# A projection kernel whose first two pairs of row tiles are loaded as four transfers of one tile each

## The chip, the core and the metric

The kernel runs on one core of a Trainium2 chip. The core has five engines that work side by side: TensorE (PE; its weight loads are shown apart as PEld), VectorE (DVE), ScalarE (ACT), GpSimd (POOL) and SyncE (SP), which here only issues transfers. Transfers are moved by 16 DMA engines that all queues of the core share. The metric is the device time of one execution in microseconds (us).

## The reference

The input x holds 16 x 512 = 8192 rows of 768 numbers, the weight `w_qkv` 768 rows of 2304 numbers, both in float32. The reference multiplies them and cuts the 2304 result columns into three parts of 768, which are stacked:

```python
qkv = np.matmul(x, w_qkv)
q, k, v = qkv[..., :768], qkv[..., 768:1536], qkv[..., 1536:]
return np.stack([q, k, v], axis=0).astype(np.float32)
```

So 25 MB of x and 7 MB of weight are read, and 75.5 MB of result are written.

## The kernel before

**Tiling.** The 8192 rows of x make 64 row tiles of 128 rows; two of them are a pair, p = 0 to 31. The contraction of 768 is cut into six slices j of 128 (`KT`), three of them being a half (`KH`). Of the 2304 result columns, two groups q = 0 and 1 have 2 x 512 columns each, and a remainder of 256 columns (`REM`) lies between them. TensorE multiplies 128 x 128 of x by 128 x 512 of weight into one bank of its accumulator memory (PSUM); there are eight banks.

**Most pairs** (2 to 31) are computed with a scheme of seven products for a 2 x 2 block matrix instead of eight, in part with float32 operands (`do`, `product`, line 247). For it x is loaded so that VectorE can turn it in blocks of 32 x 32 (`transpose`, line 155), and rounded to bfloat16 (`round_x`, `round_row`, line 203).

**Pairs 0 and 1** come first, while the weight is still arriving, and go another way. `load_rows` (line 159) loads a pair's x as it lies in memory, rows on partitions: tile `xin[p]` has 128 partitions, two row tiles r and 768 numbers of each. `cast_row` (lines 166 to 173) rounds one row tile to bfloat16, the first n columns on VectorE (line 167), the rest on ScalarE (line 168). `turn_row` turns it with six TensorE transposes (line 181), and `copy_row` (lines 188 and 190) copies a half of the turned tile from PSUM to `xb[p]`. `block` (line 485) then multiplies slice by slice: for weight slice j, the four row tiles of the two pairs, six slices for the first 512 columns and six for the next.

**Order.** The scheduling is by hand: each engine works through its instructions in the order of the program. Around the change this order is, in the program: 10 dummy matmuls on zeros (`busy(10)`, line 458); cast of pair 0's two row tiles; their transposes; a copy on VectorE; 2 dummy matmuls; cast of pair 1's two row tiles; their transposes; the cast of the first weight slice, shared by VectorE and ScalarE; copies; the cast of the second slice; more copies; casts of slices 2 to 5 on VectorE (line 465); then the first `block`.

SP issues the loads in this order: x of pair 0, x of pair 1, six weight slices of 256 KB for the first 512 columns (line 92), two weight blocks of 768 KB for the next 512, one part of pair 2's x, the remainder weight (768 KB), seven more parts of pair 2's x (line 137, 96 KB each), and more weight blocks. All of these go through one queue. The framework gives each transfer one of eight semaphores in turn, and a transfer is issued only when the one eight before it has landed. Each instruction that reads loaded data waits for the transfer that wrote that part of the tile.

Behind the first two blocks TensorE computes the remainder columns of pairs 0 and 1 (`rem`, line 310), for which VectorE and GpSimd round the remainder weight (lines 559 and 560), and then the first product of pair 2 (line 247).

Of the kernel before, what the change touches and what calls it, by code (L numbers as in the profile page):

```python
# [10 lines left out]
def kernel(  # L11
# [20 lines left out]
    nc = tc.nc  # L32
    P = 128
# [20 lines left out]
    x_flat = x.rearrange("b t h -> (b t) h")  # L54
# [66 lines left out]
    xin, xf, xb, sr = {}, {}, {}, {}  # L121
# [36 lines left out]

    def load_rows(p):
        xin[p] = xin_pool.tile([P, 2, K], fp32, name="xin")  # L160
        rows = x_flat[p * 2 * P:(p + 1) * 2 * P, :]
        nc.sync.dma_start(xin[p][:], rows.rearrange("(r m) k -> m r k", m=P))  # L162

    xc, turned_rows = {}, {}

# [274 lines left out]
    zero = xb_pool.tile([P, CB], bf16, name="zero", tag="xb")  # L440
    nc.vector.memset(zero[:], 0.0)
    load_rows(0)
    nc.scalar.activation(tiny[:], zero[:, :1], ident)
    make_identity(nc, eye)
    load_rows(1)
    load_blocks(0, 0, 1)
    load_blocks(0, 1)
# [257 lines left out]
```

## Time and profile before

Three runs took 358.91, 359.10 and 359.31 us, the median being 359.1. The profile is of the execution that took 359.31.

| what | value |
|---|---|
| time of the profiled execution | 359.31 us |
| its span (first to last instruction) | 357.5 us |
| TensorE busy | 352.4 us, 99% of the span |
| TensorE weight loads | 252.1 us, 71% |
| VectorE / ScalarE / GpSimd busy | 264.0 / 186.4 / 177.4 us |
| transfers | 108.10 MB, mean 302 GB/s |
| the two loads of pairs 0 and 1 | 768 KB each, median 4.9 us from issue to landing |
| issue of these two on SP | 0.44 and 0.45 us, from 0.74 and 1.25 us |

In the profile L162 is line 162 of the kernel. A line of the timeline gives start and length in us, engine, source line, operation, what it writes and reads, the shape and a count; in square brackets stands the idle time of the engine before it, and what ended that. In the chain that ended last, each step is the work that released the next one. A line of the table by windows gives a stretch of time and its length, the busy time and count of PE, PEld, DVE, ACT and POOL, the granted TensorE clock, the share of the DMA engines that was busy and the GB/s moved.

### The profile page before, as it was taken

The page shows a single profiled execution, that of the slowest core. Times are in us where ns is not written, and L with a number is a line of the kernel's source. Part 1 is how long each engine was busy: PE and PEld are TensorE (multiplying, and loading weights), DVE is VectorE, ACT ScalarE, POOL GpSimd, SP SyncE. Part 2 cuts the span into 40 slices and gives each one's busy share as a digit, 9 for nine tenths or more (in the row PEclk, how much of TensorE's full clock was granted, in tenths as well). Part 3 has the DMA queues.
Part 4 walks back from the last instruction along what each step waited for, and adds up shares of the span by engine and source line. Part 5 has one row for each costly group of instructions (what it writes and reads, how often), then busy time and mean ns, then how long its engine had stood idle before and what let it go on. Part 6 is the DMA issues. An engine that isn't in the chain of part 4 may idle for free.

```text
span 357.5 us, 5336 instructions
## 1 busy us (share of the span) xinstructions
PE 352.4 (99%) x1776; PEld 252.1 (71%) x1776; DVE 264.0 (74%) x309; ACT 186.4 (52%) x320; POOL 177.4 (50%) x184
## 2 busy tenths in 40 slices
PE   8999999999999999999999999999999999999996
PEld 3465577868777686877768777686877768777674
DVE  3689876796876959777695876959777695876743
ACT  5577754545454553645545454553645545454553
POOL 0031683376566353665535566353665535566320
PEclk9999999999999999999999999999999999999999
DMA  7997999998999798998979899798999979869497
GB/s 299 361 355 228 337 385 345 391 313 336 300 321 328 233 380 207 347 270 288 353 183 392 231 340 308 215 398 214 341 269 309 322 199 391 227 225 358 154 379 261
DMA packets 82075, 108.10 MB, mean 302 GB/s; under 512 B 4992, under 2 KB 62080, under 8 KB 82048
## 3 DMA queue, kind: packets, MB, share of 16 engines
q1 hardware_dynamic: 75088, 102.52, 85.7%
q10 hardware_dynamic: 6960, 5.24, 5.4%
q8 instruction: 14, 0.23, 0.3%
q14 instruction: 13, 0.11, 0.1%
HBM read 32.24 MB, written 75.50 MB: 301 GB/s over the span
## 4 chain that ended last, share of the span: by engine, by line
PE 93%; DMA 4%; SPq 1%; DVE 1%; ACT 0%; issue 0%; DVEq 0%
PE ps L247 79%; PE ps L310 11%; PE ps L485 3%; DMA xin<-in_x_dram 2%; DMA st<-in_w_qkv_dram 2%; SPq L137 1%; DVE xf L155 0%; SPq L92 0%; SPq L162 0%; ACT xb L203 0%; DVE orem L413 0%; ACT orem L412 0%; DVEq L155 0%
## 5 line engine op out<-in xcount | busy, mean ns | idle before, releaser
L247 PE MATMUL ps<-t,s 128*128 128x512 f32 x720 | 177.8, 395 | 0.0
L247 PEld LDWEIGHTS ps<-t,s 128*128 128x128 f32 x720 | 135.0, 188 | 29.6 <-ACT o L256 0.2
L155 DVE STREAM_TRANSPOSE xf<-xin 128x768 f32<-128x768 f32 (+1 forms) x45 | 93.4, 2078 | 2.7 <-DMA xin<-in_x_dram 2.6
L247 PE MATMUL ps<-b,xb 128*128 128x512 bf16 x360 | 85.4, 380 | 0.1
L287 DVE TENSOR_TENSOR o<-o,ps 128x512 f32<-128x512 f32 x56 | 38.5, 688 | 52.3 <-ACT o L286 51.7
L194 POOL CAST xb<-xf 128x1536 bf16<-128x1536 f32 x28 | 41.1, 1467 | 57.0 <-DVE xf L155 57.0
L214 POOL TENSOR_TENSOR s<-xf 128x384 fp32r<-128x384 f32 x29 | 31.0, 1067 | 72.5 <-DVE xf L155 70.8
L247 PEld LDWEIGHTS <-xb 128*128 128x128 bf16 x360 | 33.9, 98 | 37.0 <-issue 4.2
L293 DVE TENSOR_TENSOR o<-o,ps 128x512 f32<-128x512 f32 x60 | 41.2, 687 | 20.5 <-PE ps L247 19.4
L286 ACT ACTIVATE o<-ps 128x512 f32<-128x512 f32 x56 | 33.7, 601 | 41.9 <-PE ps L247 41.9
L247 PE MATMUL ps<-b,s 128*128 128x512 f32 x180 | 50.5, 389 | 0.0
L290 ACT ACTIVATE o<-ps 128x512 f32<-128x512 f32 x60 | 36.1, 601 | 25.0 <-PE ps L247 22.7
L367 DVE TENSOR_TENSOR o<-o,ps 128x512 f32<-128x512 f32 x78 | 47.8, 682 | 0.0
L310 PE MATMUL ps<-w_rem,xb 128*128 128x256 bf16 x384 | 47.5, 273 | 0.2 <-POOL w_rem L560 0.2
L275 ACT ACTIVATE o<-ps 128x512 f32<-128x512 f32 x60 | 36.1, 602 | 19.2 <-PE ps L247 13.9
L310 PEld LDWEIGHTS <-xb 128*128 128x128 bf16 x384 | 37.4, 98 | 11.9 <-issue 1.1
L324 ACT ACTIVATE orem<-ps 128x512 f32<-128x512 f32 x31 | 18.6, 598 | 48.2 <-PE ps L310 31.3
L247 PEld LDWEIGHTS ps<-b,s 128*128 128x128 f32 x180 | 33.8, 188 | 7.0
L215 POOL TENSOR_TENSOR s<-s,xf 128x384 fp32r<-128x384 f32 x29 | 29.6, 1021 | 2.3
L216 POOL TENSOR_TENSOR s<-xf 128x384 fp32r<-128x384 f32 x29 | 29.4, 1015 | 0.0
L218 POOL TENSOR_TENSOR s<-xf,s 128x384 fp32r<-128x384 f32 x29 | 29.2, 1008 | 0.0
L371 ACT ACTIVATE o<-ps 128x512 f32<-128x512 f32 x26 | 15.6, 600 | 18.1 <-PE ps L247 17.5
(51 smaller groups left out, 162.7 us busy)
## 6 DMA issues: line engine op xcount, KB each, us to landing
out_dram<-o SPq DMA_DIRECT2D x60, 768.0 KB, 4.6
out_dram<-o SPq DMA_DIRECT2D x75, 256.0 KB, 3.7
xin<-in_x_dram SPq DMA_DIRECT2D x88, 192.0 KB, 5.7
out_dram<-orem SPq DMA_DIRECT2D x31, 256.0 KB, 2.2
xin<-in_x_dram ACTq DMA_DIRECT2D x24, 192.0 KB, 4.4
st<-in_w_qkv_dram SPq DMA_DIRECT2D x5, 768.0 KB, 8.1
xin<-in_x_dram SPq DMA_DIRECT2D x2, 768.0 KB, 4.9
st<-in_w_qkv_dram SPq DMA_DIRECT2D x6, 256.0 KB, 5.9
```

The costliest lines, as they stand in the source:

```text
L155: nc.vector.transpose(turned[:, g:g + n], rows[:, g:g + n])
L194: nc.gpsimd.tensor_copy(out=xb[p][:], in_=xf[p][:])
L214: 1: lambda g: g.tensor_tensor(s[:, 1], a21, a22, op=add),
L215: 2: lambda g: g.tensor_tensor(s[:, 2], s[:, 1], a11, op=sub),
L247: nc.tensor.matmul(ps[:], lhs[j], rhs[j], start=(start and j == 0), stop=(j == KH - 1), skip_group_check=True,)
L275: nc.scalar.activation(c12, u.x[:], ident)
L286: nc.scalar.activation(c22, u.x[:], ident)
L287: nc.vector.tensor_tensor(c22, c22, u.y[:], op=add)
L290: nc.scalar.activation(c21, u.x[:], ident)
L293: nc.vector.tensor_tensor(c12, c12, u.y[:], op=add)
L310: nc.tensor.matmul(ps, xb[p][:, j, r * P:(r + 1) * P], w_rem[j // KH][:, j % KH, :], start=(j == 0), stop=(j == KT - 1), skip_group_check= ...
L367: dve.tensor_tensor(c, c, u.z[:], op=add)
```

## The change

`load_rows` issues one transfer for each of the two row tiles of a pair instead of one transfer for both. It is called for pairs 0 and 1, so that the queue begins with four transfers of 384 KB where it had two of 768 KB. The tile, its layout in memory, the bytes and the pieces of 3 KB that a row makes stay as they are; nothing else in the program is edited.

```diff
     def load_rows(p):
         xin[p] = xin_pool.tile([P, 2, K], fp32, name="xin")
-        rows = x_flat[p * 2 * P:(p + 1) * 2 * P, :]
-        nc.sync.dma_start(xin[p][:], rows.rearrange("(r m) k -> m r k", m=P))
+        for r in range(2):
+            row = (2 * p + r) * P
+            nc.sync.dma_start(xin[p][:, r], x_flat[row:row + P, :])
```

## The prediction, made before the result was known

> **What bounds the kernel now.** I read the page first, for the share of each engine:
>
> ```profile
> PE 352.4 (99%) x1776; PEld 252.1 (71%) x1776; DVE 264.0 (74%) x309; ACT 186.4 (52%) x320; POOL 177.4 (50%) x184
> ```
>
> TensorE is busy 99% of the span, so a gain must come from the few us in which it is not, or is busy with dummy work. The chain that ended last, asked for the first 24 us, says what sets the pace there:
>
> ```profile
> 2.25 5.90 DMA st<-in_w_qkv_dram
> ...
> 11.38 7.74 DMA xin<-in_x_dram
> ...
> 21.78 1.47 PE ps L247 x6
> ```
>
> The head is a transfer chain (columns: start, length, what): a weight load lands at 8.14, the queue goes on, a part of pair 2's x lands at 19.12, VectorE turns it from 19.24, ScalarE rounds it from 20.88, and at 21.78 TensorE starts pair 2. From there to the end the chain is TensorE alone, so the span of 357.5 is "when pair 2 starts" plus 335.7 us. TensorE's own timeline ahead of that point:
>
> ```profile
> 1.19 4.45 PE L458 MATMUL ps<-zero 128*128 128x512 bf16 x10 [1.19 <-DVE zero L441]
> 5.55 1.11 PE L181 MATMUL ps<-eye,xc 128*128 128x128 bf16 x12
> 6.50 0.59 PE L458 MATMUL ps<-zero 128*128 128x512 bf16 x2
> 7.39 0.85 PE L181 MATMUL ps<-eye,xc 128*128 128x128 bf16 x12 [0.30 <-ACT xc L168]
> 8.08 5.34 PE L485 MATMUL ps<-b,xb 128*128 128x512 bf16 x24
> ...
> 18.56 0.49 PE L310 MATMUL ps<-w_rem,xb 128*128 128x256 bf16 x3
> 19.25 2.45 PE L310 MATMUL ps<-w_rem,xb 128*128 128x256 bf16 x21 [0.19 <-POOL w_rem L560]
> ```
>
> The dummy matmuls end near 5.5, real ones start at 8.08 and run without a hole to 18.56; then come a wait of 0.19 for the converted remainder columns and one under 0.1 for pair 2. So the matmuls of the head also nearly touch: starting them earlier alone is worth nothing, since the remainder weight and pair 2's x hold the end of the stretch. Both must move. The other engine that matters is VectorE:
>
> ```profile
> 4.97 0.63 DVE L167 CAST xc<-xin 128x384 bf16<-128x384 f32 x2 [3.84 <-DMA xin<-in_x_dram]
> 6.36 0.36 DVE L190 COPY xb<-ps 128x384 bf16<-128x384 bf16 x1 [0.77 <-PE ps L181]
> 6.84 0.73 DVE L167 CAST xc<-xin 128x480 bf16<-128x480 f32 x2
> 7.50 0.31 DVE L167 CAST b<-st 128x288 bf16<-128x288 f32 x1
> 7.73 0.35 DVE L190 COPY xb<-ps 128x384 bf16<-128x384 bf16 x1
> ```
>
> Pair 0's x lands at 4.95 and pair 1's at 6.81. The copy at 7.73, whose end at 8.08 releases the first real matmul, stands behind the cast of the first weight slice (7.50), which starts as that slice lands. SP issues its next transfer at 7.50 too, after waiting 0.3 for the same landing. Last, transfer rates in quarter-microseconds:
>
> ```profile
> 2.00:2.25 0.25, 0.25 (x2) 0.15 (x1) 0.00 (x0) 0.22 (x2) 0.00 (x0) 1.00 0.63 221
> 2.25:2.50 0.25, 0.25 (x2) 0.06 (x1) 0.00 (x0) 0.00 (x0) 0.00 (x0) 1.00 0.55 209
> 2.50:2.75 0.25, 0.25 (x2) 0.09 (x1) 0.00 (x0) 0.00 (x0) 0.00 (x0) 1.00 0.87 258
> ...
> 33.50:33.75 0.25, 0.25 (x3) 0.11 (x2) 0.25 (x1) 0.25 (x2) 0.25 (x1) 1.00 0.88 292
> ```
>
> The last two columns are the share of the 16 DMA engines and GB/s. The first transfer needs some 0.75 us to bring the engines to 0.9; from 3 us on they are full, near 400 GB/s, until pair 2 is in.
>
> **The change, part by part.** *Transfers.* Two issues of 0.44 and 0.45 us (768 KB each) become four of 384 KB. SP's 256 KB weight loads cost about the same to issue (0.46), so I count 0.45 each with 0.05 between: SP is 1.0 us later at the first weight slice, 2.75 instead of 1.75. Cover: that slice's bytes lie behind 1.5 MB of x and flow only from about 6.8 (landing 7.48 less 0.65, the spacing of the slices), so 3.6 us remain between the end of its issue (3.2) and its turn. Without the cover it would cost the 1.0.
>
> *The queue's window.* The issues show eight transfers in flight: the ninth goes out at 4.96, just behind pair 0's landing, the tenth at 6.83 behind pair 1's, then one behind each weight slice. With four x transfers the ninth and tenth are the fifth and sixth slices, waiting for pair 0's two tiles (about 4.0 and 4.9); the two 768 KB blocks wait for pair 1's tiles (about 5.85 and 6.8). The second block so goes out as before, and pair 2's first part waits for the first slice, the remainder weight for the second, as now. All these bytes have a backlog of several us ahead of them, so nothing runs dry. Cost 0.
>
> *Landing of the tiles.* 384 KB takes about 0.95 us (pair 1 lands 1.87 behind pair 0). Row tile 0 of pair 0 lands at about 4.0 instead of 4.95, of pair 1 at 5.9 instead of 6.8; the second tiles as now. VectorE and ScalarE cast tile 0 a microsecond earlier. But the ten dummies hold TensorE until 5.43, against 5.55 for the first transpose now: 0.1 gained. Transposes of pair 1's first tile move from 7.39 to about 6.9, those of its second to about 7.3. Behind them VectorE still meets the weight slice at 7.50, and its copy still ends at 8.08. Two more casts now carry a wait of their own; what stands behind them on VectorE (the copy at 6.36) needs TensorE anyway. Gain on the path: 0. What is late next is that first weight slice.
>
> *The start of the stream.* This is the only part that can move the end, since every later landing to 19.2 follows it. Bounds: if the ramp is the time to hand out the first transfer's 256 pieces, halving it gives half the 0.9 us from the first packet to full rate, 0.45 earlier; if the ramp is a start-up of its own, 0; two more completions cost at most 0.1 (six 256 KB slices land 0.65 apart where 262,144 B at 400 GB/s need 0.655, so one completion is lost in rounding). The nearest row is the 96 KB load that meets an almost idle queue at 33.2: 128 pieces, as one tile would have, and it reaches 0.88 in about 0.5 us against 0.75. I take 0.2 earlier, between both ends.
>
> The Trainium skill ("DMA: Bandwidth & Descriptors", Rules for kernel authors and the fit in Anatomy of one DMA) says to batch transfers to 1 MiB, with about 2.0 us fixed per transfer on the software-generated path; were that paid in series here, two more transfers would give +4 us, about 363. The 0.65 spacing disagrees: the fixed part overlaps in the queue.
>
> **Sum.** The profiled execution took 359.31: 357.5 of span and 1.8 around it. Issue 0, window 0, casts 0, start of the stream -0.2; pair 2 then starts at 21.6, TensorE's 335.7 us follow. That is 359.1 against 359.31. The profiled run is the highest of the three shown, 0.2 above their median of 359.1, so I forecast 358.9.
>
> **Rivals.**
> 1. *The transfers are hidden and the stream starts as before.* For it: the later 768 KB store fills all engines quickly, so the slow ramp may belong to the first use of the queue. Time 359.1.
> 2. *The ramp goes with the number of pieces.* Then -0.45: 358.65. For it: the ramp of the 96 KB load is shorter; against: bytes per piece differ fourfold.
> 3. *Slower: TensorE's rate.* Ten dummies take 4.45 us, 24 equal matmuls at 8.08 take 5.34, so the array goes from 0.43 to 0.22 us each in this head. With earlier tiles the idle time moves: transposes, two dummies, a hole of 0.2, transposes, then 0.4 ahead of 8.08, where now there is one hole of 0.30. If that keeps the slow rate alive past 8.08, each slow matmul costs 0.21, less 0.27 for the two stalls that it eats; from five on it passes 0.2% (+0.8, about 359.9), eight give +1.4 (360.5). Against: the fast rate is there at 6.50 already, ahead of the moved holes. The Trainium skill ("TensorE: Matmul & The Clock Gate", The HAM clock gate) puts the change after a busy window of about 3.4 us and the fall back after an idle one; holes of 0.4 would not matter by it, and the row at 6.50 agrees.
> 4. *Slower: the issues reach the stream.* If SP's two further issues do delay the bytes, everything to 21.78 moves by 1.0: 360.1. It needs the 3.6 us of cover to be wrong.
> 5. *The change does not do what it says*, if the casts wait for the whole tile. The weight casts each wait for their own slice, so I expect not; 359.1 anyway.
>
> One edge lies later: ScalarE waits 2.2 us for a remainder store to land (32.9), and its backlog then reaches TensorE with almost no margin at 36 to 44 us. If TensorE comes 0.2 earlier and that landing does not, the gain is given back there (359.1); if the landing slips, up to 1 us is lost.
>
> **How the numbers follow.** Forecast (358.6 to 359.1 of its own) 0.42; rivals 1 and 5 0.27; rival 2 0.10; rival 3 0.08; rival 4 0.04; the later edge slipping 0.05; unknown 0.04, half of it faster. A measurement of this kernel tells about 0.2%, 0.7 us, from no change. Slower by more: rivals 3 and 4, part of the edge and unknown, 0.17. Faster by more needs a start 0.7 earlier than any row allows, or a lucky tail of rival 2: 0.07. Within: 0.76. The range goes from rival 2 with 0.25 for the spread of the runs, 358.4, to rival 3's point of decision, 359.9.
>
> **What would show it.** The first cast at about 4.0 or earlier; the first transpose at 5.45; SP at the first weight slice at 2.75, at pair 2's first part within 0.3 of 7.50; the first real matmul between 7.7 and 8.1; pair 2 at 21.4 to 21.8; nothing but TensorE behind. Wrong if slices land later than now, if matmuls behind 8.08 take over 0.3 us, or if new idle time appears on TensorE from 36 us on.

## The result, and the profile after

The changed kernel takes 360.65 us (median of six executions, 360.44 to 361.44) against 359.22 (six, 358.91 to 359.48): a ratio of 1.0044, 95% interval 1.0033 to 1.0055. The change costs some 1.4 us where no difference was forecast, and the time lies outside the predicted range. The profiled execution is the slowest of the six: 361.44, of which 359.7 are span, so its trace shows more than the usual loss, 2.1 us against the profiled execution of before.

The share of each engine, from the page, has hardly moved; TensorE's busy time is the same within 0.6 us (this trace holds 1757 of its 1776 matmuls):

```profile
PE 351.8 (98%) x1757; PEld 253.0 (70%) x1776; DVE 264.3 (73%) x309; ACT 186.3 (52%) x320; POOL 177.6 (49%) x184
```

The chain that ended last shows where (columns: start, length, what). It no longer goes through pair 2's x but through the weight loads:

```profile
2.60 0.43 SPq L92
...
3.08 6.92 DMA st<-in_w_qkv_dram
...
10.02 10.17 DMA str<-in_w_qkv_dram
...
20.24 1.22 POOL w_rem L561
...
21.51 2.45 PE ps L311 x21
...
24.01 1.24 PE ps L248 x5
```

SP issues the first weight slice at 2.60, a transfer chain follows until the remainder weight lands at 20.19, GpSimd rounds it, and pair 2 starts at 24.01 instead of 21.78. What follows has the very length it had before, 359.7 less 24.0 or 335.7 us, and in neither trace does TensorE wait there. (From 88 us on the chain now also names VectorE and GpSimd in places, where before it named TensorE alone; the length shows no cost of it.) So all of the loss arises ahead of 24 us. TensorE's timeline there (start, length, in square brackets the idle time before and what ended it):

```profile
1.19 4.45 PE L459 MATMUL ps<-zero 128*128 128x512 bf16 x10 [1.19 <-DVE zero L442]
5.43 1.49 PE L182 MATMUL ps<-eye,xc 128*128 128x128 bf16 x12
6.71 0.77 PE L459 MATMUL ps<-zero 128*128 128x512 bf16 x2
8.33 0.51 PE L182 MATMUL ps<-eye,xc 128*128 128x128 bf16 x6 [0.84 <-ACT xc L169]
9.28 0.51 PE L182 MATMUL ps<-eye,xc 128*128 128x128 bf16 x6 [0.44 <-ACT xc L169]
9.82 5.34 PE L486 MATMUL ps<-b,xb 128*128 128x512 bf16 x23
...
20.83 0.49 PE L311 MATMUL ps<-w_rem,xb 128*128 128x256 bf16 x3 [0.48 <-DVE w_rem L560]
```

The first transposes start at 5.43, earlier than before, but those of pair 1 wait 0.84 and 0.44 us for casts, and the first real matmul comes at 9.82 instead of 8.08. VectorE's timeline says what the casts waited for:

```profile
3.80 0.36 DVE L168 CAST xc<-xin 128x384 bf16<-128x384 f32 x1 [2.67 <-DMA xin<-in_x_dram]
4.71 0.36 DVE L168 CAST xc<-xin 128x384 bf16<-128x384 f32 x1 [0.56 <-DMA xin<-in_x_dram]
...
7.77 0.41 DVE L168 CAST xc<-xin 128x480 bf16<-128x480 f32 x1 [1.10 <-DMA xin<-in_x_dram]
8.72 0.41 DVE L168 CAST xc<-xin 128x480 bf16<-128x480 f32 x1 [0.54 <-DMA xin<-in_x_dram]
9.38 0.31 DVE L168 CAST b<-st 128x288 bf16<-128x288 f32 x1 [0.25 <-DMA st<-in_w_qkv_dram]
```

The two tiles of pair 0 arrive at 3.78 and 4.69, a little earlier than the whole of pair 0 did (4.95). The third tile, pair 1's first, comes only at 7.75, the fourth at 8.70, where the whole of pair 1 had come at 6.81; the first weight slice lands at 9.36 instead of 7.48. The reason stands in the table by windows (last columns: granted TensorE clock, share of the 16 DMA engines, GB/s), of after:

```profile
3.50:4.00 0.50, 0.50 (x3) 0.15 (x1) 0.20 (x1) 0.20 (x1) 0.00 (x0) 1.00 1.02 406
4.00:4.50 0.50, 0.50 (x2) 0.15 (x1) 0.16 (x1) 0.32 (x1) 0.00 (x0) 1.00 0.68 264
...
5.00:5.50 0.50, 0.50 (x3) 0.22 (x2) 0.07 (x1) 0.24 (x1) 0.00 (x0) 1.00 1.15 197
5.50:6.00 0.50, 0.50 (x7) 0.50 (x6) 0.00 (x0) 0.00 (x0) 0.00 (x0) 1.00 0.47 154
```

and the same stretch of before:

```profile
5.00:5.50 0.50, 0.50 (x2) 0.00 (x0) 0.50 (x2) 0.50 (x2) 0.00 (x0) 1.00 0.98 381
5.50:6.00 0.50, 0.50 (x6) 0.46 (x6) 0.10 (x1) 0.41 (x1) 0.00 (x0) 1.00 0.94 381
```

The stream is at full rate by 4.0 us and then breaks down until about 6.5. From 4.0 to 6.5 us it moved 0.61 MB where the kernel before moved 0.99, so 0.38 MB, or 0.95 us at 400 GB/s, are missing. The table counts a piece (the 3 KB of one row of x, for example) wholly in the window in which it starts, so its 1.15 and 0.47 have to be read together. Counted by the time that the pieces really fill, the 16 engines were occupied for 0.82 of these 2.5 us, before for all of it. So about half of what is missing is idle time of the engines, and the other half is pieces that took too long. Between 4.0 and 6.8 us the trace has 239 data pieces instead of 399. Their median is 121 ns in both, but nine took more than 400 ns, the longest 1304; before, none did. The landings of the 16 engines' shares of the third tile show the second part of the loss:

```
third tile, landing of each engine's share, us
5.42 5.43 5.46 5.47 5.48 5.49 5.50 5.57 5.58 5.70 5.73 6.29 6.38 6.47 6.67 7.75
```

Eleven engines are even earlier than the 5.9 predicted. One is 2 us late, and a transfer counts as landed when its last engine is through. This lag behind the next to last engine, 1.1 us here, stays at 0.7 to 0.9 us in every landing up to the second weight block's at 16.89. Loss of rate and lag together come to most of the 1.9 us by which the first weight slice is late.

### The profile page after: what moved, and what is told of

The parts are those of the page before. It is cut to its first block, busy times and chain, and to the rows that moved or that the text cites. A ratio compares the mean times of both kernels' runs of the same rounds, so it can differ in the third digit from the quotient of the medians.

```text
span 359.7 us, 5319 instructions
## 1 busy us (share of the span) xinstructions
PE 351.8 (98%) x1757; PEld 253.0 (70%) x1776; DVE 264.3 (73%) x309; ACT 186.3 (52%) x320; POOL 177.6 (49%) x184
## 3 DMA queue, kind: packets, MB, share of 16 engines
q10 hardware_dynamic: 6960, 5.24, 5.4%
## 4 chain that ended last, share of the span: by engine, by line
PE 70%; POOL 15%; DVE 6%; DMA 5%; issue 3%; SPq 1%; ACT 0%
PE ps L248 56%; PE ps L311 12%; DVE xf L155 5%; POOL xb L195 5%; POOL s L216 3%; POOL s L215 3%; POOL s L217 3%; PE ps L486 3%; DMA str<-in_w_qkv_dram 3%; DMA st<-in_w_qkv_dram 2%; SPq L163 0%; POOL w_rem L561 0%; DVE o L294 0%; SPq L92 0%; DVE orem L414 0%
## 5 line engine op out<-in xcount | busy, mean ns | idle before, releaser
L248 PE MATMUL ps<-b,xb 128*128 128x512 bf16 x343 | 81.5, 379 | 1.1
```

The costliest lines, as they stand in the source:

```text
L248: nc.tensor.matmul(ps[:], lhs[j], rhs[j], start=(start and j == 0), stop=(j == KH - 1), skip_group_check=True,)
```

## The experiments

Each is compared with the kernel before on the same chip. Names in capitals are the theories that the expectations weigh: PLACE, that the third transfer finds the engines short of work, whatever it is; SUPPLY, the same for two short transfers ahead of it; BACKLOG, that the transfers queued behind x get in its way; PATTERN, that the order in which a short transfer reads memory is to blame; COUNT, that there are more transfers; CASTS, that casts now run while x still arrives; ISSUE, that SP issues during these microseconds; CUSHION, that a stream which opens with short transfers stalls, and that a long one at its head prevents it.

### Which pair matters

The split for one pair alone.

```diff
-        rows = x_flat[p * 2 * P:(p + 1) * 2 * P, :]
-        nc.sync.dma_start(xin[p][:], rows.rearrange("(r m) k -> m r k", m=P))
+        if p == 0:
+            for r in range(2):
+                row = (2 * p + r) * P
+                nc.sync.dma_start(xin[p][:, r], x_flat[row:row + P, :])
+        else:
+            rows = x_flat[p * 2 * P:(p + 1) * 2 * P, :]
+            nc.sync.dma_start(xin[p][:], rows.rearrange("(r m) k -> m r k", m=P))
```

> Only pair 0 is loaded as two transfers of one row tile; pair 1 stays one transfer of 768 KB. In the changed kernel the first two tiles landed at 3.78 and 4.69 us and the third only at 7.75 instead of about 5.7. Theory PLACE (the third transfer, wanted at about 4.1 us, finds the engines short of work whatever it is): pair 1 lands 1 to 2 us late, at 7.5 to 8.5 instead of 6.6, and the time is 360 to 361. Theory PATTERN (a transfer of 128 rows that follow each other in memory is what stalls, in pair 1): as before, 358.8 to 359.3, pair 1 lands at 6.5 to 6.8. Theory COUNT (each additional transfer at the head of the queue costs its share): about 359.9, pair 1 at 7.2 to 7.5.

Measured: 361.56 us against 358.84, ratio 1.0060 (1.0028 to 1.0092). The five executions fall into two groups, 361.56 to 362.24 and 359.43 to 359.64. In the profiled one, of the upper group, pair 0's tiles land at 4.03 and 4.92; of pair 1's single transfer 15 engines are through by 6.90 and one at 8.69, after a piece that took 1125 ns at 5.10. So splitting pair 0 is enough for the whole loss, as PLACE had it, and the two groups suggest that it strikes in some executions and much less in others. In this trace nearly all of it is the lag of one engine: from 4.0 to 6.5 us the stream moved 0.95 MB, almost what it moved before.

The other pair, with `p == 1` in place of `p == 0`:

> Only pair 1 is loaded as two transfers of one row tile; pair 0 stays one of 768 KB. PLACE: the third transfer, pair 1's second tile, is wanted at about 5.2 us, and a second stands ready for the engines from 4.2; little or no stall, 359.0 to 359.6, tiles of pair 1 at 5.9 and 6.9. PATTERN: the stall of about 2 us is all here, 360.4 to 361.4, second tile at 8 to 8.7. COUNT: 359.9, second tile at 7.2 to 7.5.

Measured: 359.2 us, ratio 1.0006 (0.9997 to 1.0016): no difference. The tiles land at 4.95, 5.86 and 6.81, the first slice at 7.51. TensorE's timeline of this kernel:

```profile
7.09 0.85 PE L186 MATMUL ps<-eye,xc 128*128 128x128 bf16 x12
7.97 5.34 PE L490 MATMUL ps<-b,xb 128*128 128x512 bf16 x24
...
21.21 1.47 PE L252 MATMUL ps<-b,xb 128*128 128x512 bf16 x6
```

Transposes and matmuls follow each other without a wait, pair 2 starts at 21.21, and pair 1 lands as predicted for it (5.9, 6.8). The pair whose landing suffered in the changed kernel is not the pair whose split does the harm. With three transfers of x in both kernels, COUNT can't tell the one from the other.

### The pattern in memory

Four transfers of the same size, each of 64 partitions and both row tiles, so that the data come in the order of the kernel before.

```diff
-        rows = x_flat[p * 2 * P:(p + 1) * 2 * P, :]
-        nc.sync.dma_start(xin[p][:], rows.rearrange("(r m) k -> m r k", m=P))
+        rows = x_flat[p * 2 * P:(p + 1) * 2 * P, :].rearrange("(r m) k -> m r k", m=P)
+        for h in range(2):
+            n = slice(h * P // 2, (h + 1) * P // 2)
+            nc.sync.dma_start(xin[p][n], rows[n])
```

> Four transfers of 384 KB as in the changed kernel, but each holds 64 partitions of both row tiles instead of 128 partitions of one, so a transfer's pieces of 3 KB alternate between two stretches of memory as before the change. The casts of a pair wait for both of its transfers. PLACE and COUNT: the third transfer lands near 7.7 again, the time is 360.4 to 361.4. PATTERN: no stall, second pair complete at 6.5 to 6.9, 358.8 to 359.4.

Measured: 364.75 us, ratio 1.0151 (1.0123 to 1.0179). It answers another question than it was made for. The four land at 5.36, 7.09, 8.86 and 10.60, each 1.74 us behind the other. One line of its windows:

```profile
4.50:5.00 0.50, 0.50 (x2) 0.15 (x1) 0.00 (x0) 0.00 (x0) 0.00 (x0) 1.00 0.98 233
```

The engines are as busy as can be, at half the rate: a piece of 3 KB takes 233 ns (median) instead of 121. That is no stall, and a cost of its own that covers whatever else there was. The Trainium skill ("SBUF — State Buffer", Door 1: The DMA port swizzle) says that the bandwidth of a transfer depends on how many of the 16 memory ports its partitions reach, and by its formula 64 partitions in a row reach eight. The halved rate agrees with it. No run here shows the ports themselves.

So a second try, with the split by tile of the changed kernel but rows read in steps of two. Its expectation says which results this permutes.

```diff
-        rows = x_flat[p * 2 * P:(p + 1) * 2 * P, :]
-        nc.sync.dma_start(xin[p][:], rows.rearrange("(r m) k -> m r k", m=P))
+        rows = x_flat[p * 2 * P:(p + 1) * 2 * P, :].rearrange("(m r) k -> r m k", r=2)
+        for r in range(2):
+            nc.sync.dma_start(xin[p][:, r], rows[r])
```

> Four transfers of one tile of 128 partitions as in the changed kernel, but a tile takes every second row of the pair (the first tile the even rows), so the rows that a transfer reads do not follow each other in memory. Within pairs 0 and 1 the output rows so stand in another order; the work is the same. PATTERN: no stall, tiles at about 3.8, 4.7, 5.7 and 6.6, 358.6 to 359.3. PLACE and COUNT: as the changed kernel, third tile near 7.7, 360.4 to 361.4.

Measured: 361.01 us, ratio 1.0054 (1.0039 to 1.0069), the changed kernel's loss. Tiles at 3.90, 4.79, 6.86 and 8.52, with pieces of up to 1325 ns between 4.3 and 6.9 us. PATTERN falls, as far as this order can tell.

### Casts beside the stream

In the changed kernel the first cast starts at 3.80, just ahead of the break at 4.0. Here the second tile's cast stands first, so that both wait for 4.7.

```diff
-    for r in range(2):
+    for r in (1, 0):
         cast_row(0, r, K // 2)
...
-    for r in range(2):
+    for r in (1, 0):
         cast_row(1, r, 480)
```

> As the changed kernel, but the casts of a pair begin with its second tile, so VectorE and ScalarE read nothing before that has landed: first cast at about 4.7 us instead of 3.8. Theory CASTS (the early casts, which begin in the three slow kernels just before the transfers stall at 4.0 to 4.4 us, disturb them): the stall begins later or is gone, third tile at 5.7 to 6.3, 358.7 to 359.6. Theory SUPPLY (the engines, done with two short transfers at 4.1 us, want a third one's pieces before these stand ready): no difference to the changed kernel, third tile at 6.8 to 7.8, 360.2 to 361.4.

Measured: 361.6 us against 358.92, ratio 1.0079 (1.0058 to 1.0101). VectorE's first cast of this kernel:

```profile
4.72 0.63 DVE L168 CAST xc<-xin 128x384 bf16<-128x384 f32 x2 [3.59 <-DMA xin<-in_x_dram]
```

and three of its windows:

```profile
4.00:4.50 0.50, 0.50 (x2) 0.15 (x1) 0.00 (x0) 0.00 (x0) 0.00 (x0) 1.00 1.02 277
...
10.00:10.50 0.50, 0.50 (x7) 0.50 (x6) 0.00 (x0) 0.50 (x2) 0.00 (x0) 0.50 1.06 410
...
13.00:13.50 0.50, 0.50 (x4) 0.23 (x3) 0.00 (x0) 0.00 (x0) 0.00 (x0) 1.00 1.04 406
```

The rate breaks at 4.0 (277 GB/s) although no cast runs until 4.72; tiles at 3.80, 4.70, 6.70, 8.27. CASTS falls. The other two windows show something else: the granted clock is halved from 9.25 to 12.67 us, and the first 24 real matmuls take 6.47 us instead of 5.34, so 1.1 us of this execution's loss is not the stream's. The four executions agree with that: two with a mean granted clock of 0.999 and 1.000 took 361.05 and 361.02 us, two with 0.995 took 362.15 and 362.72. More on the clock below.

The counterpart, the kernel before with useless casts from the start on, did not do what it was made for.

```diff
     busy(10)
+    spare = both[:, 1, :K // 2]
+    nc.vector.memset(spare, 0.0)
+    left = both[:, 0, :K // 2].bitcast(bf16)
+    for _ in range(10):
+        nc.vector.tensor_copy(out=left[:, :K // 2], in_=spare)
+    for _ in range(6):
+        nc.scalar.activation(left[:, K // 2:], spare, ident)
```

> The kernel before with ten useless casts of 128x384 on VectorE and six on ScalarE ahead of the first real casts, so that both engines are busy from 1.4 and 2.2 us to 4.2 and 4.8. CASTS: the transfers stall at some point between 2 and 5 us, pair 0 or pair 1 lands 0.5 to 2 us late, 359.5 to 361. SUPPLY: as before, pairs at 4.95 and 6.8, 358.7 to 359.4.

Measured: 380.56 us against 358.92, ratio 1.0607 (1.0586 to 1.0627). The tile that they write is one that a weight load also writes, so they waited for that load and ran at 22 us, and everything behind them with them. They also overwrite a part of that weight block, so the results of its columns are not those of the reference. The transfers landed as before (4.99, 6.91), with no cast beside them. It says nothing on CASTS.

### What stands behind x in the queue

The changed kernel, with everything behind x issued only once the third tile's cast is done.

```diff
+            if held:
+                nc.vector.memset(t[:, 0, :1], 0.0)
...
-    for r in range(2):
-        cast_row(1, r, 480)
+    cast_row(1, 0, 480)
+    load_blocks(0, 0, 1, held=True)
+    load_blocks(0, 1)
+    load_x_rows(2, (0, ))
...
+    cast_row(1, 1, 480)
```

> As the changed kernel, but nothing is queued behind the four x transfers until pair 1's first tile has been cast (the first weight slice waits for a one-column memset behind that cast). If the transfers queued behind them (theory BACKLOG: SP's issues from 2.6 to 6.3 us, three of which take 0.65 to 0.8 instead of 0.43, get in the way of the x transfers) make the stall: third tile at 5.6 to 5.8, fourth at 6.5 to 6.8, and the weights, issued at 6.1, land from 7.8 on, so 359.4 to 360.2. CASTS and SUPPLY: third tile still at 6.8 to 7.8; the weights then land from 9.5 on, 360.8 to 362.

Measured: 364.02 us against 358.92, ratio 1.0141 (1.0124 to 1.0158); the weights come late here by the edit itself. What it was made for is the landings: 3.81, 4.96, 6.12, 7.06, and the longest piece between 4 and 7 us took 614 ns. Two windows, to be held against the 197 and 154 GB/s of the changed kernel:

```profile
5.00:5.50 0.50, 0.50 (x4) 0.23 (x3) 0.34 (x1) 0.50 (x1) 0.00 (x0) 1.00 1.01 350
5.50:6.00 0.50, 0.50 (x12) 0.50 (x11) 0.04 (x1) 0.01 (x1) 0.00 (x0) 1.00 0.99 393
```

From 4.0 to 6.0 us the stream runs at 338 to 393 GB/s, and the third tile is only 0.2 later than predicted. The landings lie between what BACKLOG had forecast (5.6 to 5.8 and 6.5 to 6.8) and the others' 6.8 to 7.8, nearer to BACKLOG: most of the stall is gone when SP issues nothing behind the four short transfers. The weights then open a new stream in an empty queue at 6.68, again with short transfers, and that stalls in its turn: slices at 9.42 and 10.03, then the third, whose engines are through from 10.47 to 11.77, and the fourth, from 11.11 to 12.89.

The kernel before with the weight slices issued late, while pair 1 is still flowing (eight small VectorE writes into their tile hold them):

```diff
-    def load_blocks(q, c, nj=KH):
+    def load_blocks(q, c, nj=KH, held=0):
...
+            for _ in range(held):
+                nc.vector.memset(t[:, 0, :384], 0.0)
...
-    load_blocks(0, 0, 1)
+    load_blocks(0, 0, 1, held=8)
```

> The kernel before, two whole transfers, but SP issues the weight slices only from about 3.9 us on (eight useless memsets of VectorE on the slices' tile hold them), so that it hands them out until 6.8 us, while pair 1 flows. ISSUE: pair 1 or the first slices land 1 to 2 us late with some engines far behind. CUSHION: pair 0 at 4.95 and pair 1 at 6.8 as before, slices 0.65 apart from 7.5 on, nothing lost.

Measured: 362.36 us beside 359.19, one execution of each. The issues ran from 5.24 to 8.97, later than meant. While they began, from 5.0 to 6.0 us, pair 1 flowed on at 406 to 412 GB/s, and it landed at 6.87 as before, so an issue by SP did not by itself disturb a running stream. But behind pair 1 only the slices that SP had just issued, from 5.24 us on, were left:

```profile
6.50:7.00 0.50, 0.50 (x4) 0.02 (x1) 0.17 (x2) 0.11 (x1) 0.00 (x0) 1.00 0.92 102
```

Here too the pieces that start (a share of 0.92) move only 102 GB/s; they take up to 876 ns, and counted by the time that they fill the engines are occupied for 0.64 of the window. That is the same picture as in the changed kernel, in a place where short transfers follow close behind their own issue. The landings were neither theory's: pair 1 came as CUSHION had it, the first slice at 8.63.

### A long transfer at the head

Now the opposite: the changed kernel, with a weight block of 768 KB, needed later anyway, issued ahead of x.

```diff
+    t01 = tq_pool.tile([P, KT, CB], fp32, name="st0", tag="tq")
+    load_w(t01[:, :KH], 0, KH, Q_OFF[0] + CB, CB)
+    stage[0, 0, 1], stage[0, 1, 1] = t01[:, :KH, :], t01[:, KH:, :]
     load_rows(0)
...
-    load_blocks(0, 1)
+    load_w(t01[:, KH:], KH, KH, Q_OFF[0] + CB, CB)
```

> As the changed kernel, but one 768 KB weight half (which the kernel needs later anyway) is issued ahead of the four tiles, so that the stream begins with a long transfer; all of x comes 1.9 us later, and the time rises for that alone. The question is the spacing of the landings. Theory CUSHION (the stall needs a stream that begins with short transfers, so that the engines follow closely behind what SP has handed out): the four tiles land 0.9 to 1.0 us apart, at about 5.9, 6.8, 7.8 and 8.7, and no engine is late by over 0.6. Theory ISSUE (whatever flows while SP hands out its sixth to tenth transfer, at 4.0 to 6.3 us, stalls): first or second tile 1 to 2 us late, one engine or several far behind the others.

Measured: 362.8 us beside 359.19, one execution. The block lands at 5.86, the four tiles at 6.76, 7.70, 8.70 and 9.63, the slices about 0.65 apart behind them. No piece takes more than 121 ns from 4 to 14 us. But x comes 2.8 us later than in the kernel before (pairs complete at 7.70 and 9.63), not the 1.9 expected, and the first of the real matmuls run at half the rate, which is a part of the 3.6 us that this execution takes longer.

The same edit with x whole (the kernel before plus the long transfer) and once more with x split, timed side by side:

> The kernel before with one edit: a 768 KB weight block, the first half of the second 512 columns, is issued ahead of x, and x of pairs 0 and 1 stays two transfers of 768 KB. It is the partner of e12, which differs only in that x is four transfers. x arrives some 1.9 us later than in the kernel before, so the time is about 362 to 363. CUSHION (the stall strikes a stream that opens with short transfers): landings 5.9, 7.8, 9.7, no hole in the stream behind 4 us. COUNT (four x transfers are what stalls): the same here; the two differ in e12.

> The same large weight block first, then x as four transfers of 384 KB. CUSHION: with a long transfer ahead the split costs nothing: the four tiles land 0.93 to 1.0 apart, the time is within 0.2% (0.7 us) of e11_large_first_x_whole, and no execution is 1 us above its fellows. COUNT or a cost of the split itself: the third or fourth tile is late by 1 to 2 us as in the changed kernel, and the time is 1 us or more above e11_large_first_x_whole in most executions.

Measured: 362.16 us whole (361.50 to 363.02), ratio to before 1.0097 (1.0078 to 1.0115); 361.77 split (361.04 to 362.81), ratio 1.0080 (1.0060 to 1.0100). The split is 0.4 us below the whole in the medians, within the spread of both; that spread, 1.5 and 1.8 us, is wider than CUSHION had it, and with four executions of each a cost below about 1 us would not show in the times. Three windows of the split one:

```profile
2.50:3.00 0.50, 0.50 (x3) 0.23 (x2) 0.00 (x0) 0.00 (x0) 0.00 (x0) 1.00 0.74 184
...
5.00:5.50 0.50, 0.00 (x0) 0.00 (x0) 0.00 (x0) 0.00 (x0) 0.00 (x0) 1.00 1.05 422
5.50:6.00 0.50, 0.00 (x0) 0.00 (x0) 0.00 (x0) 0.00 (x0) 0.00 (x0) 1.00 1.06 424
```

From 4.0 to 7.0 us the stream runs at 399 to 424 GB/s, the tiles land at 6.65, 7.59, 8.58 and 9.54, and five transfers lie ahead of the first slice where the changed kernel has four. COUNT falls, and no cost of the split as such is to be seen behind the long transfer. But look at the first line: this kernel has its slow pieces too, up to 1026 ns, only in the first 4 us, while the long transfer is under way. The kernel with x whole has them there as well (865 ns). The block itself landed at 5.73 with x split behind it and at 5.44 with x whole, one trace of each, and the pairs of x 0.3 to 0.4 us later. A long transfer at the head does not do away with the slow pieces; they fall into it, and the tiles behind it come evenly.

### The changed kernel again

> The changed kernel once more, for a second look at the stall: the first two tiles at 3.7 to 3.9 and 4.6 to 4.8 us, the third at 6.5 to 8 with a spread of over 0.9 us between the first and the last of the 16 engines. If the same share of engines is late, the cause lies in their places; if another, in the timing of the run.

Measured: 361.9 us beside 359.19, one execution. Tiles at 3.72, 5.61, 7.80 and 8.80. This time one engine is already late for the second tile (5.61, the others by 4.64) and two for the third (7.77 and 7.80, the others 5.39 to 6.95). How many engines are late, and from which tile on, changes from execution to execution, which speaks for the timing of the run; which engines they are the trace does not say. Pair 2 starts at 24.47.

## Why the prediction was wrong

**Transfers: right.** SP reached the first weight slice at 2.60 (predicted 2.75). The cover of 3.6 us was there, and rival 4, whose 1.0 us would have looked much like the result, is not what happened.

**The queue's window: the step that failed.** The order was as predicted: the fifth and sixth slice went out behind pair 0's tiles (at 4.90 and 5.59, some 0.8 us later than predicted), the two blocks behind pair 1's at 7.76 and 8.71, pair 2's part behind the first slice. But "nothing runs dry. Cost 0" was wrong. I took bytes that SP had issued for bytes that the engines work on at full rate. At 4.0 us the four tiles and three slices had been issued, and yet from 4.0 to 6.5 us the engines were occupied for 0.82 of the time only, and some of their pieces took up to ten times as long. The term put at 0 was 0.95 us of missing rate and 0.8 us of one engine's lag.

**Landing of the tiles: right for pair 0, wrong for pair 1.** 3.78 and 4.69 against 4.0 and 4.9 predicted; then 7.75 and 8.70 against 5.9 and 6.8. "What is late next is that first weight slice" named the right place, with a wrong time: the slice was predicted where it was, at 7.5, and came at 9.36.

**The start of the stream: right in this execution, and worth nothing.** The second tile, which completes pair 0, came 0.26 us earlier than pair 0 had (predicted 0.2). That is partly luck: in the other traces that open with a split pair 0 it came between 4.70 and 5.61. The bounds of this term, -0.45 to +0.1, were the trouble: the upper one came from slices in the midst of a full queue. A row from a stream that had just opened was there, the slow first 0.75 us, and I read it as something that a smaller transfer could only shorten. I also read the 96 KB load at 33.2 by the engines' share (0.88) and not by the rate. A quarter of a microsecond earlier the kernel before has:

```profile
33.25:33.50 0.25, 0.25 (x2) 0.10 (x1) 0.25 (x1) 0.25 (x2) 0.25 (x1) 1.00 0.74 108
```

The engines look busy there, 0.74, and move 108 GB/s, against 292 at 0.88 in the row that the prediction shows: the picture of the changed kernel on a small scale.

**The sum.** TensorE's 335.7 us from pair 2 on held to the tenth, and pair 2 started at 24.0 instead of 21.6; the median of the executions is 1.4 us above the kernel before. The sign that the prediction gave for its being wrong, slices that land later than now, is the one that came.

**The rivals.** None of them was this. Rival 3 did not take place in the changed kernel: matmuls behind 9.82 are 0.216 us apart and the granted clock reads 1.00, with holes of 0.84 and 0.44 us ahead of them. The later edge at 36 to 44 us did not show either.

What is shown: the loss needs pair 0 split (the first two experiments), the tiles come evenly with a long transfer ahead of the same four, and it is not the order in memory, the casts or the number of transfers. SP's further issues alone do not do it either: behind the long transfer SP issued from 4.22 to 5.17 us beside a stream of 412 to 422 GB/s. But they seem to be the other half of the cause, since without them (the weights held back) most of the stall was gone, one trace. So what stalled is a stream of short transfers that had just been opened, while SP went on issuing. Not shown is why a piece then takes up to 1.3 us. SP's issues in that stretch took 0.65 to 0.81 us instead of 0.43; whether they slow the pieces, or the pieces slow them, or both have a third cause, is open.

## What to carry to other kernels

Cut transfers behind a long one, not at the head of a stream: the same split cost nothing for pair 1 and some 1.4 us where it opened the queue. The Trainium skill ("Perfetto Trace Analysis", DMA Optimizations) says that splitting may let some transfers start sooner; the first tile here did land 1.2 us sooner, and everything from the third tile on came later. When a cost is bounded from rows of a stream at full rate, ask whether the change acts while the stream is being started, and take the bound from there; read a rate in GB/s and not in the share of busy engines; and read a landing as that of the slowest of 16 engines.

## What the runs showed of the hardware that was not expected

The lag of one engine is not made up within a full queue: 0.82 us at the first weight slice, 0.75 at the first block 5 us later.

A transfer to 64 partitions ran at half the rate with all engines busy (215 to 246 GB/s, a median of 233 ns for 3 KB).

TensorE's clock, which the prediction's rival 3 was about, shows up in six of the experiments. In five traces the granted clock fell back to 0.50 in the head, after it had risen: at 9.25 us where the second tile was cast first, at 8.70 with the partition halves, at 8.50 with the useless casts, and at 7.26 and 7.46 with the long transfer ahead, x whole and x split. With the partition halves the first 24 real matmuls so took 6.85 us instead of 5.34. In the single execution with the long transfer ahead the matmuls kept the slow spacing of 0.43 us until 13.3 us (the view prints 1.00 ahead of the first change on record, so there the spacing is the better witness). A line of each kind, the slow matmuls of that execution and a window of the one with x whole:

```profile
11.07 6.46 PE L489 MATMUL ps<-b,xb 128*128 128x512 bf16 x23
...
9.00:9.50 0.50, 0.50 (x5) 0.32 (x3) 0.43 (x2) 0.30 (x1) 0.00 (x0) 0.50 1.05 406
```

Each fall came 3.41 us after the clock had risen, and the low clock lasted 3.41 us, or 6.83 with the partition halves and 20.48 with the useless casts, twice and six times as long. In the 3.41 us ahead of the five falls TensorE was busy for 0.34 to 1.28 us. With pair 0 alone split the clock stayed up through idle time of 2.78 us; counted in steps of 3.41 from its rise at 4.01, that idle time falls into two steps, in which TensorE was busy for 2.19 and 1.56 us. So these traces fit a clock that is decided anew every 3.41 us by how long TensorE worked, with a limit for staying up between 1.28 and 1.56 us; that is worked out from these few cases and no more. The Trainium skill ("TensorE: Matmul & The Clock Gate", The HAM clock gate) has the clock fall after an idle window of about 3.4 us that runs on its own, whatever the kernel does. The length agrees; that the window must be idle does not, with up to 1.28 us of work in it.
